# Last expert's down product and scatter, the gate half summed first, and the column offsets of the big tiles

## The chip, the cores and the metric

The kernel runs on one core of a Trainium2 chip. The metric is the device time of one execution in microseconds (us), lower being better. The kernel before was run three times: median 1566.77 us, from 1564.66 to 1566.87.

## The reference

One transformer block over a sequence of S = 256 rows with D = 2048 columns, all in fp32. A first part mixes a gated spatial unit and forgetting attention and adds its projection to the input; a second adds a mixture of experts. What matters here is the second:

```python
def hierarchical_moe(h, w_rg, b_rg, w_re, b_re, w_g, w_u, w_d):
    ...
    # one of 4 groups per row, then the best 2 of its 8 experts,
    # with gates w_top = softmax(top_v) * p_grp
    ...
    def expert_block(args):
        xi, e = args
        return (jax.nn.silu(xi @ w_g[e]) * (xi @ w_u[e])) @ w_d[e]
    ...
    y = y.at[buf_tok].add(yb * buf_gate[:, None])
```

There are 32 experts; `w_g` and `w_u` are 2048 x 512 each and `w_d` is 512 x 2048, so one expert has 12 MB of weights and all of them some 400 MB. Each row of the input goes to two experts and their results are added, times the row's gates.

## The kernel before, in words

The program has three stages, which are called the front, the expert stage and the tail below.

**The front** computes everything up to the router with products in split fp32r. `half` (L221 to L241) takes one weight tile of 128 partitions x 8 x 512, which a DMA of 2 MB brought, and for each of its eight 512-column slices makes a high part on ACT (L230) and the rest on DVE (L231). The two go by turns to a pair of 512-column tiles, either `wh` and `wl` or a pair cut out of the tile `ex` (`split_tiles`, L145). For each slice and each of the two 128-row blocks of the sequence TensorE makes three matmuls: high by high (L236), high by low (L237) and low by high (L238). The weights' part is what moves through TensorE, 512 columns at a time, and the 128x128 piece that is held comes from `hT`, `so` or `mT`, the transposed activations in split form. The profile calls the products `z<-wh,hT`, `z<-wl,hT`, `z<-ex,hT` and so on. The last projection goes in 256-column pieces.

Tiles are taken from pools on two sides of SBUF. On the left lie the two weight tiles `w0` and `w1` (the profile's `w`), the split tiles `wh` and `wl` and later `rb`; on the right `hT0`, `hT1`, `so0`, `so1`, `third`, `ex`, `bm`, `mT0`, `mT1`. In the built program each tile on the left begins at byte 416 of a 512-byte line (address modulo 512), each on the right at byte 480. The activations `x1`, which are read in the expert stage, begin at byte 128.

**The expert stage** streams the experts' weights, six tiles of 2 MB for each (two of gate, two of up, two of down), through the big tiles of the front as slots as these come free. `load` (L541) issues the next transfer on SP's queue whenever a slot is handed back: `used_up` is called after the last matmul that reads a slot. The loop over the experts is at L1020. For each, `hidden` makes the gate half and then the up half (16 matmuls each, four of them side by side in four column groups of the array, L861), `gather` prepares the next expert's rows, `silu_mul` (L866) copies the two results out of PSUM (gate on ACT, up on DVE, 512 columns each), sums and turns them by eight matmuls against `four` (L879), and makes `h` by a tanh on ACT and two DVE products (L881 to L884). `down` (L887) multiplies by the down weights, and after each fourth expert `scatter` (L997) adds the four results to the rows of the output `acc`, by a matmul against a 0/gate matrix `gt` and an addition on DVE. If some expert has more rows than its 32 places, `overflow` (L925) makes further passes; SP reads the number of those, `novi`, into a register for it.

**The tail** treats the last expert's down product apart. Its weights come in five column blocks, LAST = (0, 512), (512, 512), (1024, 512), (1536, 256), (1792, 256) as first column and width, each cut out of the usual rows of `w_expert_down`. `columns` (L903) makes the four partial products of a block (L908) and copies them to `yl` on ACT (L912), `add_columns` (L915) sums and spreads them by one fp32 matmul for each of the two row blocks (L920) against a matrix that holds the gates (`gq`, from `one_gates`, L845), and DVE adds the result to `acc` (L922). Then the block goes out. `keep_warm` (L158) issues matmuls on a constant, in numbers that the table WARM sets: WARM[1] = 20 of them before the last four matmuls of the last up half, WARM[2] = 10 behind it, WARM[3] = 10 before the first column block.

PE, DVE and ACT each run their instructions in the order that a scheduler wrote for them, SP its transfers likewise.

Of the kernel before, what the change touches and what calls it, by code (L numbers as in the profile page):

```python
# [9 lines left out]
F32 = mybir.dt.float32  # L10
F32R = mybir.dt.float32r
BF16 = mybir.dt.bfloat16
I32 = mybir.dt.int32
# [30 lines left out]
def hybrid_block(ctx: ExitStack, tc: tile.TileContext, a, out, dbg=None):  # L44
# [61 lines left out]
    def early(pool, name, dt=F32R):  # L106
        return pool.tile([P, QW], dt, tag=name, name=name)

    def wide_tile(pool, name, dt=F32R):
        return pool.tile([P, HW], dt, tag=name, name=name)  # L110

    def halves(pool, name):

# [427 lines left out]
    def load(n=1):  # L541


        while n and free and order:
            n -= 1
            t = order.popleft()
            slot[t] = free.popleft()
            w = slot[t][0]
            e, m, c = t // 6, t // 2 % 3, t % 2
            src = a[names[m]][e * P:(e + 1) * P]  # L550
            if t < last:
                n0 = HW // len(w)
                for i, wi in enumerate(w):
                    nc.sync.dma_start(wi, src[:, c * HW + i * n0:c * HW + (i + 1) * n0])
            else:
                sv = src.rearrange("p (j n) -> p j n", j=4)
                for c0, n0 in LAST:
                    if c0 // 1024 == c:
                        wv = quarter(t, c0 // 512 % 2).rearrange("p (j n) -> p j n", j=4)
                        nc.sync.dma_start(wv[:, :, c0 % 512:c0 % 512 + n0], sv[:, :, c0:c0 + n0])  # L560

    def quarter(t, c):

        w = slot[t][0]
        return w[c] if len(w) == 2 else w[0][:, c * QW:(c + 1) * QW]

    def room(tiles, keep=True):

# [258 lines left out]
    def turned(eq, tag):  # L827
# [4 lines left out]
        gt = mo.tile([P, S], F32, tag=tag, name="gt")  # L832
        nc.vector.tensor_copy(gt, gt_ps[:, :S])
        return gt

# [9 lines left out]
    def one_gates(pos, g, tag):  # L845

        eq = mo.tile([P, NT, 4, CAP], F32, tag="eq", name="eq")
        for tb in range(NT):
            ts(eq[:, tb], iota1.unsqueeze(1).to_broadcast([P, 4, CAP]), pos(tb), g(tb), ALU.is_equal, ALU.mult)
        return turned(eq, tag)  # L850

    def hidden(xT, t, piece=None):

        ps = gup.tile([P, 512], F32, tag="gu", name="ps")
        for c in range(4):
            if piece is None and t == last - 2 and c == 3:
                keep_warm(WARM[1])
            w = quarter(t + c // 2, c % 2) if piece is None else piece(c)
            w = w.rearrange("p (i d) -> p i d", i=4)
            for i in range(4):  # L860
                nc.tensor.matmul(ps[32 * i:32 * i + 32], xT[:, i, c], w[:, i], start=(c == 0), stop=(c == 3))  # L861
            if piece is None and c % 2:
                used_up(t + c // 2)
        return ps

    def silu_mul(g_ps, u_ps):  # L866


        s_ps = trm.tile([P, 512], F32, tag="tr", name="s_ps")
        both = []  # L870
        for i, ps in enumerate((g_ps, u_ps)):
            q = mo.tile([P, 512], F32, tag="xg", name="q")
            if i:
                nc.vector.tensor_copy(q, ps)  # L874
            else:
                nc.scalar.activation(q, ps, AF.Copy)
            both.append(s_ps[:, i * P:(i + 1) * P])
            for j in range(4):
                nc.tensor.matmul(both[i][:, j * CAP:(j + 1) * CAP], q[:, j * P:(j + 1) * P], four, start=True, stop=True)  # L879
        t = mo.tile([P, P], F32, tag="th", name="t")  # L880
        nc.scalar.activation(t, both[0], AF.Tanh, scale=0.5)  # L881
        stt(t, t, 1.0, both[0], ALU.add, ALU.mult)
        h = mo.tile([P, 4, CAP], F32, tag="h", name="h")
        stt(h.rearrange("p a b -> p (a b)"), t, 0.5, both[1], ALU.mult, ALU.mult)  # L884
        return h

    def down(h, t, p0):  # L887
# [12 lines left out]
            else:  # L900
                nc.vector.tensor_copy(o, i)  # L901

    def columns(h, w, tag):  # L903
# [5 lines left out]
        yl = mo.tile([P, 512], F32, tag=tag, name="yl", bufs=2 if tag == "xT" else 1)[:, :n]  # L909
        m = min(n, 256)  # L910
        for i in range(0, n, m):
            nc.scalar.activation(yl[:, i:i + m], y_ps[:, i:i + m], AF.Copy)  # L912
        return yl

    def add_columns(yl, gq, c0):  # L915

        n = yl.shape[1]
# [27 lines left out]
    def overflow_block(base, cum, ix, piof):  # L945
# [40 lines left out]
                return wo  # L986
            return f

        h = silu_mul(*(hidden(xo, None, piece(n)) for n in names[:2]))
        for c in range(4):  # L990
            wv = wo.rearrange("p (j n) -> p j n", j=4)
            for j in range(4):
                rows(wv[:, j], a["we_d"].rearrange("r (k n) -> (r k) n", n=512), row[:, 1 + j, c:c + 1])
            add_columns(columns(h, wv, "xg"), gq, c * 512)
        ts(ix, ix, 1.0, None, ALU.add)

    def scatter(q, gt, c):  # L997
# [22 lines left out]
    for e in range(NE):  # L1020
        q, el = divmod(e, 4)
        xT, t = nxt, 6 * e
        g_ps = hidden(xT, t)
        u_ps = hidden(xT, t + 2)
        if el == 0:
            gt = group_gates(q)
        if e < NE - 1:
            nxt = gather(e + 1)
        else:
            gq = one_gates(lambda tb: pos1[:, tb, e:e + 1], lambda tb: gw[:, tb, e:e + 1], "gq")  # L1030
            nc.gpsimd.memset(y[3 * CAP:], 0.0)
# [10 lines left out]
    yl = None  # L1042
    for i in range(len(LAST) + 1):
        nxt = None
        if i < len(LAST):
            c0, n = LAST[i]
            w = quarter(last + c0 // 1024, c0 // 512 % 2).rearrange("p (j n) -> p j n", j=4)[:, :, c0 % 512:c0 % 512 + n]
# [8 lines left out]
        yl = nxt  # L1056

def layout(inputs):  # L1060
# [19 lines left out]
    g0 = 5 * SW + NH  # L1080
    for n in range(4):
        order += [w[:, g0 + n * 512:g0 + (n + 1) * 512], w[:, g0 + D + n * 512:g0 + D + (n + 1) * 512]]
    wp = np.concatenate([g["w_proj_sgu"][0], g["w_proj_fox"][0]], axis=0)
    return {
        "x": c(x.reshape(NT, P, D).transpose(1, 0, 2)),
# [38 lines left out]
```

## Time and profile before

| what | value |
|---|---|
| median of three runs | 1566.77 us |
| the profiled execution | 1564.82 us |
| its span, first to last instruction | 1563.1 us |
| PE busy in the span | 1331.6 us (85%) |
| DVE busy | 578.4 us (37%) |
| ACT busy | 405.7 us (26%) |
| DMA rate over the span | 335 GB/s |
| mean granted TensorE clock | 0.916 |

The span is what the trace shows; the time of an execution is 1.7 us more than it. A busy share is an average over the three stages, which have different limits, so each stage is to be read by itself.

### The profile page before, as it was taken

What the parts mean: (1) busy time and instruction counts of PE and PEld (TensorE: products, weight loads), DVE (VectorE), ACT (ScalarE), POOL (GpSimd) and SP (SyncE); (2) the same over time, 40 slices, a digit from 0 to 9 for tenths busy, and PEclk for the clock granted to TensorE, in tenths of its full rate; (3) what the DMA queues carried; (4) which work ended last, traced back from release to release, by engine and by line L of the source; (5) the groups of instructions that cost most, each with busy time, mean ns of one, the idle gap of its engine ahead of it and who ended that gap; (6) DMA issues with size and microseconds to landing.
All of it is one profiled execution on the core that took longest, in us unless ns stands there. A gap on an engine that the chain in (4) does not pass through costs nothing. (4 is left out here: it accounts for less than half of the span.)

```text
span 1563.1 us, 18318 instructions
## 1 busy us (share of the span) xinstructions
PE 1331.6 (85%) x7506; PEld 749.6 (48%) x7506; DVE 578.4 (37%) x1089; ACT 405.7 (26%) x724; POOL 31.9 (2%) x38
## 2 busy tenths in 40 slices
PE   9999999999999999898766878768778668768667
PEld 7787888888888878533222322222222212222223
DVE  6766766655655655422112202112112112112112
ACT  6645455545445444111000100010010000000000
POOL 0300100000000000000000000000000000000000
PEclk9999999999999999999788979789778888889889
DMA  9554453455555955899999999999999999999996
GB/s 384 223 209 169 161 201 142 155 200 192 199 192 223 369 228 190 347 425 428 425 426 425 425 428 426 427 426 427 426 426 426 425 428 426 426 427 426 427 425 240
DMA packets 50375, 523.53 MB, mean 335 GB/s; under 512 B 5872, under 2 KB 11632, under 8 KB 16752
## 3 DMA queue, kind: packets, MB, share of 16 engines
q1 hardware_dynamic: 48992, 520.22, 80.7%
q10 hardware_dynamic: 1296, 2.11, 0.5%
q8 instruction: 60, 0.98, 0.2%
q14 instruction: 27, 0.22, 0.0%
HBM read 520.21 MB, written 2.10 MB: 334 GB/s over the span
## 5 line engine op out<-in xcount | busy, mean ns | idle before, releaser
L231 DVE TENSOR_TENSOR wl<-w,wh 128x512 fp32r<-128x512 f32 x220 | 151.0, 690 | 115.2 <-ACT wh L230 114.8
L230 ACT ACTIVATE wh<-w 128x512 fp32r<-128x512 f32 x220 | 138.0, 631 | 157.0 <-PE z L238 145.3
L874 DVE COPY q<-ps 128x512 f32<-128x512 f32 x32 | 22.1, 692 | 391.4 <-PE ps L861 385.3
L236 PE MATMUL z<-wh,hT 128*128 128x512 f32 x382 | 153.3, 402 | 0.8 <-ACT wh L230 0.8
L237 PE MATMUL z<-wl,hT 128*128 128x512 f32 x382 | 151.1, 396 | 2.3 <-DVE wl L231 2.3
L238 PE MATMUL z<-wh,hT 128*128 128x512 f32 x382 | 150.8, 395 | 0.0
L879 PEld LDWEIGHTS s_ps<-four,q 128*128 128x128 f32 x512 | 70.9, 214 | 117.7 <-DVE q L874 63.5
L879 PE MATMUL s_ps<-four,q 128*128 128x32 f32 x512 | 78.2, 300 | 46.5 <-DVE q L874 25.5
L899 ACT ACTIVATE mT<-y_ps 32x512 f32<-32x512 f32 x62 | 36.5, 589 | 278.3 <-DVE mT L901 278.3
L861 PE MATMUL ps<-hT,xT 128*32 128x512 f32 x512 | 76.6, 711 | 33.3 <-DMA hT<-in_we_u_dram 17.1
L861 PE MATMUL ps<-w,xT 128*32 128x512 f32 x512 | 80.1, 747 | 27.4 <-DMA w<-in_we_u_dram 22.7
L881 ACT ACTIVATE t<-s_ps 128x128 f32<-128x128 f32 x32 | 8.9, 278 | 320.8 <-PE s_ps L879 320.8
L816 PE MATMUL x_ps<-x,sel 128*32 128x512 f32 x512 | 90.1, 708 | 0.7 <-DVE sel L812 0.7
L237 PEld LDWEIGHTS z<-wl,hT 128*128 128x128 f32 x382 | 71.7, 188 | 19.9 <-DVE wl L231 4.2
L901 DVE COPY mT<-y_ps 32x512 f32<-32x512 f32 x62 | 42.4, 684 | 103.7 <-PE y_ps L892 83.4
L236 PEld LDWEIGHTS z<-wh,hT 128*128 128x128 f32 x382 | 71.6, 188 | 17.7 <-ACT wh L230 1.0
L238 PEld LDWEIGHTS z<-wh,hT 128*128 128x128 f32 x382 | 71.6, 187 | 17.2
L861 PE MATMUL ps<-third,xT 128*32 128x512 f32 x320 | 53.8, 740 | 26.7 <-DMA third<-in_we_u_dram 15.3
L236 PE MATMUL z<-ex,hT 128*128 128x512 f32 x194 | 76.4, 395 | 0.0
L237 PE MATMUL z<-ex,hT 128*128 128x512 f32 x194 | 76.0, 392 | 0.0
L238 PE MATMUL z<-ex,hT 128*128 128x512 f32 x194 | 75.8, 391 | 0.0
L861 PE MATMUL ps<-so,xT 128*32 128x512 f32 x352 | 56.0, 745 | 21.4 <-DMA so<-in_we_g_dram 19.0
(301 smaller groups left out, 1852.9 us busy)
## 6 DMA issues: line engine op xcount, KB each, us to landing
w<-in_we_u_dram SPq DMA_DIRECT2D x21, 2048.0 KB, 34.3
w<-in_w_in_dram SPq DMA_DIRECT2D x20, 2048.0 KB, 7.4
hT<-in_we_u_dram SPq DMA_DIRECT2D x20, 2048.0 KB, 34.3
so<-in_we_d_dram SPq DMA_DIRECT2D x20, 2048.0 KB, 34.3
third<-in_w_in_dram SPq DMA_DIRECT2D x14, 2048.0 KB, 7.3
hT<-in_we_g_dram SPq DMA_DIRECT2D x12, 2048.0 KB, 34.3
so<-in_we_u_dram SPq DMA_DIRECT2D x12, 2048.0 KB, 36.8
w<-in_we_g_dram SPq DMA_DIRECT2D x11, 2048.0 KB, 34.3
```

The source lines that it names most:

```text
L230: nc.scalar.activation(wh, wv, AF.Copy)
L231: nc.vector.tensor_tensor(wl, wv, wh.bitcast(F32), ALU.subtract)
L236: nc.tensor.matmul(z[tb], hi, wh[:, i - j], start=first, stop=False)
L237: nc.tensor.matmul(z[tb], hi, wl[:, i - j], start=False, stop=False)
L238: nc.tensor.matmul(z[tb], lo, wh[:, i - j], start=False, stop=final)
L816: nc.tensor.matmul(x_ps[32 * c:32 * c + 32], sel[:, tb], x1[:, tb, c * 512:(c + 1) * 512], start=(tb == 0), stop=(tb == NT - 1))
L861: nc.tensor.matmul(ps[32 * i:32 * i + 32], xT[:, i, c], w[:, i], start=(c == 0), stop=(c == 3))
L874: nc.vector.tensor_copy(q, ps)
L879: nc.tensor.matmul(both[i][:, j * CAP:(j + 1) * CAP], q[:, j * P:(j + 1) * P], four, start=True, stop=True)
L881: nc.scalar.activation(t, both[0], AF.Tanh, scale=0.5)
L899: nc.scalar.activation(o, i, AF.Copy)
L901: nc.vector.tensor_copy(o, i)
```

## The change

It has four parts.

1. The last expert's down weights come from a new array, `we_l`, which the host lays out so that each column block's row lies in one piece (8 KB or 4 KB for each partition, where it was four pieces of 2 KB or 1 KB).
2. For every expert the gate half is copied out, summed, turned and put through tanh ahead of the up half. Each half is copied by both engines, columns 0 to 255 by ACT and the rest by DVE. `group_gates` and the last `one_gates` move; the 20 constant matmuls inside the last up half and the 10 behind it go, and 6 stay ahead of the first column block.
3. In the tail a block's partial products are split into an fp32r high part (ACT) and the rest (DVE) in a tile `fine`, which takes the place of a slot, and two fp32r matmuls for each row block take the place of one in fp32. The matrix holds ones; the gate is applied where DVE adds to `acc`.
4. Two unused tiles of 8 fp32 (`pad`, `rpad`) are put in and `ii` gets its place in `low`. In the built program all big tiles, on both sides, then begin at byte 448 of a 512-byte line; `x1` stays at 128.

The number of experts' transfers, their size, the matmuls of the front and their order on every engine are the same as before.

```diff
-WARM = (45, 20, 10, 10, 4, 60, 0)
+WARM = (45, 20, 0, 6, 4, 60, 0)
...
+    ctile([P, 8], F32, "pad")
...
     bm = early(ra, "bm", F32)
+    ra.tile([P, 8], F32, tag="rpad", name="rpad")
...
-    ii = small.tile([P, CAP], I32, tag="ii", name="ii", bufs=1)
+    ii = low.rearrange("p a b -> p (a b)")[:, 0:CAP].bitcast(I32)
...
-                        wv = quarter(t, c0 // 512 % 2).rearrange("p (j n) -> p j n", j=4)
-                        nc.sync.dma_start(wv[:, :, c0 % 512:c0 % 512 + n0], sv[:, :, c0:c0 + n0])
+                        nc.sync.dma_start(block(c0, n0), a["we_l"][:, 4 * c0:4 * (c0 + n0)])
...
-            if piece is None and t == last - 2 and c == 3:
-                keep_warm(WARM[1])
...
+    def add_turned(o, ps):
+
+        q = mo.tile([P, 512], F32, tag="xg", name="q")
+        nc.scalar.activation(q[:, 0:256], ps[:, 0:256], AF.Copy)
+        nc.vector.tensor_copy(q[:, 256:], ps[:, 256:])
+        for j in range(4):
+            nc.tensor.matmul(o[:, j * CAP:(j + 1) * CAP], q[:, j * P:(j + 1) * P], four, start=True, stop=True)
...
+    def silu(g_ps):
 
         s_ps = trm.tile([P, 512], F32, tag="tr", name="s_ps")
...
+        g = s_ps[:, 0:P]
+        add_turned(g, g_ps)
         t = mo.tile([P, P], F32, tag="th", name="t")
+        nc.scalar.activation(t, g, AF.Tanh, scale=0.5)
+        stt(t, t, 1.0, g, ALU.add, ALU.mult)
+        return t, s_ps[:, P:2 * P]
+
+    def times_up(tu, u_ps):
+        t, u = tu
+        add_turned(u, u_ps)
         h = mo.tile([P, 4, CAP], F32, tag="h", name="h")
+        stt(h.rearrange("p a b -> p (a b)"), t, 0.5, u, ALU.mult, ALU.mult)
         return h
...
-    def add_columns(yl, gq, c0):
+    def add_columns(parts, gq, c0, gate=None):
...
-            keep(nc.tensor.matmul(ps, gq[:, tb * P:(tb + 1) * P], yl, start=True, stop=True))
+            for i, yl in enumerate(parts):
+                keep(nc.tensor.matmul(ps, gq[:, tb * P:(tb + 1) * P], yl, start=(i == 0), stop=(i == len(parts) - 1)))
             o = acc[tb][:, c0:c0 + n]
-            tt(o, o, ps, ALU.add)
+            if gate is None:
+                tt(o, o, ps, ALU.add)
+            else:
+                stt(o, ps, gate(tb), o, ALU.mult, ALU.add)
...
-        g_ps = hidden(xT, t)
+        if e == NE - 1:
+            gq = one_gates(lambda tb: pos1[:, tb, e:e + 1], None, "gq", F32R)
+            nc.gpsimd.memset(y[3 * CAP:], 0.0)
+        tu = silu(hidden(xT, t))
         u_ps = hidden(xT, t + 2)
-        if el == 0:
-            gt = group_gates(q)
...
-        h = silu_mul(g_ps, u_ps)
+        h = times_up(tu, u_ps)
+        if el == 0:
+            gt = group_gates(q)
...
-            nxt = columns(h, w, "xT")
+            y_ps = columns(h, block(c0, n).rearrange("p (j n) -> p j n", j=4))
+            nxt = [fine[:, 2 * c0 + k * n:2 * c0 + (k + 1) * n] for k in range(2)]
+            nc.scalar.activation(nxt[0], y_ps, AF.Copy)
+            tt(nxt[1], y_ps, nxt[0].bitcast(F32), ALU.subtract)
...
-            add_columns(yl, gq, c0)
+            add_columns(parts, gq, c0, lambda tb: gw[:, tb, NE - 1:NE])
...
+        "we_l": c(np.concatenate([wl[:, :, i:i + n].reshape(P, 4 * n) for i, n in LAST], axis=1)),
```

The order of SP's transfers at the start of the expert stage, where the first experts' weights are fetched. Before:

```order
L554 DMA w_121<-in_we_u_dram 128x4096
L554 DMA rb<-in_we_u_dram 128x4096
L554 DMA mT_5259<-in_we_d_dram 128x4096
L554 DMA hT_4181<-in_we_d_dram 128x4096
L554 DMA hT_4182<-in_we_g_dram 128x4096
```

And after:

```order
L561 DMA w_123<-in_we_u_dram 128x4096
L561 DMA rb<-in_we_u_dram 128x4096
L561 DMA mT_5260<-in_we_d_dram 128x4096
L942 TENSOR_LOAD novi
L942 ISA x2
L561 DMA hT_4182<-in_we_d_dram 128x4096
L561 DMA hT_4183<-in_we_g_dram 128x4096
```

The load of `novi` into a register, which stood 44 rows further down, ahead of a transfer to `third`, now stands ahead of the first transfer to `hT`.

DVE's last instructions, from the last expert's sums on. Before, the tail has two additions for each column block:

```order
L833 COPY gt<-gt_ps 128x256
L874 COPY q<-ps 128x512
L882 SCALAR_TENSOR_TENSOR t<-t,s_ps 128x128
L884 SCALAR_TENSOR_TENSOR h<-t,s_ps 128x128
L922 TENSOR_TENSOR mT_5066<-mT_5066,ps 128x512
L922 TENSOR_TENSOR mT_5259<-mT_5259,ps 128x512
```

And after, with `hT_9178` the tile `fine`, `mT_5067` and `mT_5260` the two row blocks of the output:

```order
L882 COPY q<-ps 128x256
L900 SCALAR_TENSOR_TENSOR h<-t,s_ps 128x128
L1073 TENSOR_TENSOR hT_9178<-y_ps,hT_9178 128x512
L938 SCALAR_TENSOR_TENSOR mT_5067<-ps,gw,mT_5067 128x512
L1073 TENSOR_TENSOR hT_9178<-y_ps,hT_9178 128x512
L938 SCALAR_TENSOR_TENSOR mT_5260<-ps,gw,mT_5260 128x512
L938 SCALAR_TENSOR_TENSOR mT_5067<-ps,gw,mT_5067 128x512
L1073 TENSOR_TENSOR hT_9178<-y_ps,hT_9178 128x512
L938 SCALAR_TENSOR_TENSOR mT_5260<-ps,gw,mT_5260 128x512
```

Each block has three DVE instructions in place of two, and those before `h` have become a copy of half the width and one product.

## Rows read from the trace of the kernel before

**Rows 1.** Busy time by stretch; columns as in the first line.

```profile
core 0: us, PE busy (x) PEld busy (x) DVE busy (x) ACT busy (x) POOL busy (x), PEclk, DMA share, GB/s
0.00:640.00 640.00, 633.39 (x3060) 513.36 (x3061) 396.02 (x717) 321.90 (x557) 30.07 (x37) 1.00 0.57 218
640.00:1536.00 896.00, 677.29 (x4313) 226.72 (x4317) 174.85 (x360) 80.73 (x158) 1.80 (x1) 0.86 1.00 423
...
1546.00:1548.00 2.00, 2.00 (x11) 0.34 (x11) 0.00 (x0) 0.01 (x1) 0.00 (x0) 0.50 0.02 5
```

**Rows 2.** Chain that ended last, in order of time: start us, us, what.

```profile
1501.35 34.41 DMA w<-in_we_u_dram
...
1535.80 1.06 PE ps L861 x8
1536.87 1.22 PE ps L158 x20
...
1542.73 1.09 PE s_ps L879 x8
...
1546.06 1.86 PE y_ps L908 x8
...
1549.44 1.91 PE ps L920 x4
1551.35 1.00 PE y_ps L908 x8
...
1559.69 0.42 DVE mT L922
```

**Rows 3.** Timeline around the front's end and SP's queue: start us, us, instruction.

```profile
643.20 0.15 DVE L1018 CAST novi<-nov 128x1 int32<-128x1 f32 x1
647.34 0.33 SPq L554 DMA_DIRECT2D hT<-in_we_d_dram  x1
...
810.60 0.33 SPq L554 DMA_DIRECT2D so<-in_we_u_dram  x1
813.13 0.33 SPq L554 DMA_DIRECT2D third<-in_we_u_dram  x1
```

**Rows 4.** Timeline of PE in the front, products from both kinds of split tile.

```profile
200.06 0.39 PE L236 MATMUL z<-wh,hT 128*128 128x512 f32 x1
...
203.56 0.39 PE L236 MATMUL z<-ex,hT 128*128 128x512 f32 x1
...
204.94 0.39 PE L236 MATMUL z<-ex,hT 128*128 128x512 f32 x1
...
206.30 0.39 PE L236 MATMUL z<-wh,hT 128*128 128x512 f32 x1
```

**Rows 5.** Front's first product by tile and shape: count, busy us, mean ns, idle before.

```profile
L236 PE MATMUL z<-wh,hT 128*128 128x512 f32 x382 | 153.3, 402 | 0.8 <-ACT wh L230 0.8
L236 PE MATMUL z<-ex,hT 128*128 128x512 f32 x194 | 76.4, 395 | 0.0
L236 PE MATMUL z<-wh,mT 128*128 128x512 f32 x88 | 35.6, 405 | 0.0
L236 PE MATMUL z<-wh,so 128*128 128x512 f32 x88 | 34.7, 394 | 0.0
...
L236 PE MATMUL z<-ex,so 128*128 128x512 f32 x40 | 15.6, 390 | 0.0
```

**Rows 6.** Timeline of weight loads in a scatter of the expert stage, one per matmul.

```profile
956.50 0.19 PEld L1001 LDWEIGHTS ps<-mT,gt 128*128 128x128 f32 x1 [0.24 <-issue]
956.93 0.19 PEld L1001 LDWEIGHTS ps<-mT,gt 128*128 128x128 f32 x1 [0.24 <-issue]
```

**Rows 7.** A DVE copy of 256 columns in the tail, from the timeline.

```profile
1539.49 0.42 DVE L833 COPY gt<-gt_ps 128x256 f32<-128x256 f32 x1 [7.87 <-PE gt_ps L831]
```

**Rows 8.** Groups by shape: instructions of 512 columns from PSUM to fp32r.

```profile
L530 DVE SCALAR_TENSOR_TENSOR mT<-ps,mT 128x512 fp32r<-128x512 f32 x8 | 5.5, 684 | 0.0
L529 ACT ACTIVATE mT<-ps 128x512 fp32r<-128x512 f32 x8 | 4.7, 583 | 0.0
```

More of the change, by code (lines that the diff above doesn't have):

```diff
@@ L107, in early @@
         return pool.tile([P, QW], dt, tag=name, name=name)
+    home = {}
     def wide_tile(pool, name, dt=F32R):
-        return pool.tile([P, HW], dt, tag=name, name=name)
+        t = pool.tile([P, HW], dt, tag=name, name=name)
+        home[id(t)] = pool, name
+        return t
     def halves(pool, name):
@@ L565, in quarter, with block @@
         return w[c] if len(w) == 2 else w[0][:, c * QW:(c + 1) * QW]
+    def block(c0, n0):
+        o = c0 % 512
+        return quarter(last + c0 // 1024, c0 // 512 % 2)[:, 4 * o:4 * (o + n0)]
     def room(tiles, keep=True):
@@ L825, in gather, with turned @@
         return xT
-    def turned(eq, tag):
+    def turned(eq, tag, dt=F32):
         gt_ps = trm.tile([P, 512], F32, tag="tr", name="gt_ps")
@@ L831, in turned @@
             nc.tensor.transpose(gt_ps[:, tb * P:(tb + 1) * P], eq[:, tb].rearrange("p a b -> p (a b)"), ident)
-        gt = mo.tile([P, S], F32, tag=tag, name="gt")
+        gt = mo.tile([P, S], dt, tag=tag, name="gt")
         nc.vector.tensor_copy(gt, gt_ps[:, :S])
@@ L843, in group_gates, with one_gates @@
         return turned(eq, "gt")
-    def one_gates(pos, g, tag):
+    def one_gates(pos, g, tag, dt=F32):
         eq = mo.tile([P, NT, 4, CAP], F32, tag="eq", name="eq")
         for tb in range(NT):
-            ts(eq[:, tb], iota1.unsqueeze(1).to_broadcast([P, 4, CAP]), pos(tb), g(tb), ALU.is_equal, ALU.mult)
-        return turned(eq, tag)
+            i1 = iota1.unsqueeze(1).to_broadcast([P, 4, CAP])
+            if g is None:
+                ts(eq[:, tb], i1, pos(tb), None, ALU.is_equal)
+            else:
+                ts(eq[:, tb], i1, pos(tb), g(tb), ALU.is_equal, ALU.mult)
+        return turned(eq, tag, dt)
     def hidden(xT, t, piece=None):
@@ L864, in hidden @@
         return ps
-    def silu_mul(g_ps, u_ps):
-        s_ps = trm.tile([P, 512], F32, tag="tr", name="s_ps")
[L870 to L879, printed above, removed]
-        t = mo.tile([P, P], F32, tag="th", name="t")
-        nc.scalar.activation(t, both[0], AF.Tanh, scale=0.5)
-        stt(t, t, 1.0, both[0], ALU.add, ALU.mult)
+    def add_turned(o, ps):
[5 more added lines that the diff above has]
+    def silu(g_ps):
+        s_ps = trm.tile([P, 512], F32, tag="tr", name="s_ps")
+        g = s_ps[:, 0:P]
+        add_turned(g, g_ps)
+        t = mo.tile([P, P], F32, tag="th", name="t")
+        nc.scalar.activation(t, g, AF.Tanh, scale=0.5)
[4 more added lines that the diff above has]
+        add_turned(u, u_ps)
         h = mo.tile([P, 4, CAP], F32, tag="h", name="h")
-        stt(h.rearrange("p a b -> p (a b)"), t, 0.5, both[1], ALU.mult, ALU.mult)
+        stt(h.rearrange("p a b -> p (a b)"), t, 0.5, u, ALU.mult, ALU.mult)
         return h
@@ L901, in down, with columns @@
                 nc.vector.tensor_copy(o, i)
-    def columns(h, w, tag):
+    def columns(h, w):
         n = w.shape[2]
@@ L908, in columns @@
             keep(nc.tensor.matmul(y_ps[32 * j:32 * j + 32], h[:, j], w[:, j], start=True, stop=True))
[L909 to L913, printed above, removed]
-    def add_columns(yl, gq, c0):
-        n = yl.shape[1]
+        return y_ps
+    def add_columns(parts, gq, c0, gate=None):
+        n = parts[0].shape[1]
         for tb in range(NT):
             ps = scm.tile([P, 512], F32, tag="sc", name="ps")[:, :n]
-            keep(nc.tensor.matmul(ps, gq[:, tb * P:(tb + 1) * P], yl, start=True, stop=True))
+            for i, yl in enumerate(parts):
+                keep(nc.tensor.matmul(ps, gq[:, tb * P:(tb + 1) * P], yl, start=(i == 0), stop=(i == len(parts) - 1)))
             o = acc[tb][:, c0:c0 + n]
-            tt(o, o, ps, ALU.add)
+            if gate is None:
+                tt(o, o, ps, ALU.add)
+            else:
+                stt(o, ps, gate(tb), o, ALU.mult, ALU.add)
     def overflow():
@@ L987, in piece @@
             return f
-        h = silu_mul(*(hidden(xo, None, piece(n)) for n in names[:2]))
+        tu = silu(hidden(xo, None, piece(names[0])))
+        h = times_up(tu, hidden(xo, None, piece(names[1])))
         for c in range(4):
@@ L993, in overflow_block @@
                 rows(wv[:, j], a["we_d"].rearrange("r (k n) -> (r k) n", n=512), row[:, 1 + j, c:c + 1])
-            add_columns(columns(h, wv, "xg"), gq, c * 512)
+            yo = mo.tile([P, 512], F32, tag="xg", name="yo")
+            nc.scalar.activation(yo, columns(h, wv), AF.Copy)
+            add_columns([yo], gq, c * 512)
         ts(ix, ix, 1.0, None, ALU.add)
@@ L1029, in hybrid_block @@
         else:
-            gq = one_gates(lambda tb: pos1[:, tb, e:e + 1], lambda tb: gw[:, tb, e:e + 1], "gq")
-            nc.gpsimd.memset(y[3 * CAP:], 0.0)
             keep_warm(WARM[2])
-        h = silu_mul(g_ps, u_ps)
+        h = times_up(tu, u_ps)
+        if el == 0:
+            gt = group_gates(q)
         if e < NE - 1:
@@ L1041, in hybrid_block @@
     keep_warm(WARM[3])
-    yl = None
+    pool, tag = home[id(slot[6 * (NE - 2) + 3][0][0])]
+    fine = wide_tile(pool, tag, F32R)
+    parts = None
     for i in range(len(LAST) + 1):
@@ L1046, in hybrid_block @@
             c0, n = LAST[i]
-            w = quarter(last + c0 // 1024, c0 // 512 % 2).rearrange("p (j n) -> p j n", j=4)[:, :, c0 % 512:c0 % 512 + n]
-            nxt = columns(h, w, "xT")
+            y_ps = columns(h, block(c0, n).rearrange("p (j n) -> p j n", j=4))
+            nxt = [fine[:, 2 * c0 + k * n:2 * c0 + (k + 1) * n] for k in range(2)]
+            nc.scalar.activation(nxt[0], y_ps, AF.Copy)
+            tt(nxt[1], y_ps, nxt[0].bitcast(F32), ALU.subtract)
             if i == 0:
@@ L1052, in hybrid_block @@
             c0, n = LAST[i - 1]
-            add_columns(yl, gq, c0)
+            add_columns(parts, gq, c0, lambda tb: gw[:, tb, NE - 1:NE])
             for tb in range(NT):
                 nc.sync.dma_start(out[tb * P:(tb + 1) * P, c0:c0 + n], acc[tb][:, c0:c0 + n])
-        yl = nxt
+        parts = nxt
 def layout(inputs):
@@ L1082, in layout @@
         order += [w[:, g0 + n * 512:g0 + (n + 1) * 512], w[:, g0 + D + n * 512:g0 + D + (n + 1) * 512]]
+    wl = g["w_expert_down"][0][NE - 1].reshape(4, P, D).transpose(1, 0, 2)
     wp = np.concatenate([g["w_proj_sgu"][0], g["w_proj_fox"][0]], axis=0)
```

1 line of the change is left out of this document (removed).

## The prediction, made before the changed kernel had run

> **What bounds the kernel now.** I read the busy time by stretch first, then the chain of waits backwards from the end. Up to 640 us PE is busy for 633.4 us at a granted clock of 1.00 while the DMA engines are busy 0.57 of the time: the front is bound by TensorE [rows 1]. From 640 to 1536 us DMA is busy all the time at 423 GB/s and PE only 677 of 896 us: the expert stage is bound by the stream of weights. The chain says the same: it steps from transfer to transfer, the last taking 34.41 us from its issue at 1501.35, since it stands behind some seven others, 2.097 MB / 423 GB/s = 4.96 us each [rows 1, 2]. That tile is the last up tile. It lands at 1535.76, and what follows is a chain of small steps on PE, ACT and DVE that ends with an addition at 1559.69 + 0.42 = 1560.11: the tail [rows 2]. The span ends 3.0 us behind that, with the last output transfer, which the change leaves as it is.
>
> So three things can move the time: PE's pace in the front, the start of the stream, and the length of the tail. Time saved on PE or DVE inside the expert stage is not seen.
>
> **The expert stage: nothing.** Summing the gate first puts a copy and four small matmuls between the two halves. That delays the release of an up tile by about a copy of 256 columns and half of a 1.09 us sum, some 1 us [rows 2, 7]; the cover is the queue of about 34 us [rows 2]. Without that cover it would be 1 us for each of 32 experts. One thing changes at the start: the load of `novi` goes ahead of the first transfer to `hT` on SP. `novi` is ready at 643.35 and that transfer starts at 647.34, so it has 4.0 us [rows 3]. In the old place the load and its branches stand between two issues that are 2.53 us apart [rows 3], and that bounds it. Cost 0, from 0 to 0.5. Everything behind it on SP, the whole stream, would be late by what it exceeds.
>
> **The tail: -8.3 us.** By the new order, from the landing at 1535.76:
> - the last up half, 16 matmuls as two groups of 1.06 without the 20 constant ones (1.22) between them: 1535.8 + 2.1 = 1537.9 [rows 2];
> - its copy, now 256 columns on each engine, 0.42: 1538.3 [rows 7]; the sum 1.09: 1539.4 [rows 2]; one DVE product of 128 columns, at most the copy's 0.4: 1539.8. Tanh and the first product are already done with the gate half;
> - 6 constant matmuls at 1.22 / 20 = 0.06: 1540.2; the first column block 1.00, as the second took at full clock [rows 2]: 1541.2;
> - ACT's high part, 0.58: 1541.8 [rows 8].
> From there DVE sets the pace. It has 3 instructions for each of three 512-column blocks at 0.684 and for each of two 256-column blocks at 0.42: 6.2 + 2.5 = 8.7 [rows 7, 8]. I add 0.7 for the first matmuls between its first subtraction and its first addition, and 15 hand-overs of 0.04 (an estimate from the gap between 1535.76 and 1535.80). The last addition ends at 1541.8 + 8.7 + 0.7 + 0.6 = 1551.8, against 1560.11: -8.3. PE needs 1.00 + 4 x 0.23 = 1.9 us for a wide block, just less than DVE's 2.05 [rows 2, 4, 8].
>
> The blocks' weights must not be late: 4 MB behind 1535.76 at 423 GB/s land at 1538.2, 1540.7 and 1543.2 for the wide ones [rows 1], and the first is wanted at 1540.2, the second at 1541.2. That is 0.5 us of cover; if packets of longer rows gain nothing, up to 1 us is lost. Bounds of the tail: -9.5 if the hand-overs cost nothing and copies overlap more, -4 if the clock falls (rival D).
>
> **The front: -11.2 us.** No instruction moves, but the tiles do: the moving operand `wh`, `wl` goes from byte 416 of its line, `ex` and the held `hT`, `so`, `mT` from 480, all to 448. The trace shows two paces. From 200.06 to 203.56 stand 15 matmuls from `wh` and `wl`: 233.3 ns each. From 204.94 to 206.30 stand 6 from `ex`: 226.7 ns [rows 4]. PE has no idle time to speak of beside them [rows 5], so pace is time. The slower kind are (382 + 88 + 88) x 3 = 1674, the faster (194 + 40) x 3 = 702 [rows 5]. What distinguishes the two is that `ex` lies at the same offset as the operand that is held, and `wh` does not, 64 bytes away. If the common offset is the cause, all run at 226.7 after the change: 1674 x 6.67 = 11.2 us less. The stream then starts earlier by as much, since its first transfer to `hT` waits for the front. No row shows a tile at 448, so the effect is bounded by the nearest rows: nothing if the two paces belong to the tiles and not to offsets, a step of 6.67 ns more (240) or less (220) either way, and below that the pace of the fp32 rows. I take 226.7, as that is the one row of a pair with equal offsets.
>
> An fp32 matmul of the expert stage, whose moving `mT` lies at 480 too, follows the one before it in 0.43 us, which is 214.5 for each time that 512 columns pass if they pass twice [rows 6]. By the Trainium skill, "TensorE: Matmul & The Clock Gate", section "Back-to-back issue gap", 512 columns take 512 / 2.4 + 2.5 = 216 ns alone and some 131 ns in a stream with weight loads. The trace disagrees with both: 233.3 and 226.7 in just such a stream. By 216 the front could get about 36 us shorter, an estimate from that page and the counts, which would be the direction of rival B. Against it speaks that the fp32 rows have their pace without any change of offset.
>
> **Sum.** 1564.82 - 8.3 - 11.2 = 1545.3 for an execution like the profiled one. The median of the three runs is 1.95 above that execution, so 1547.3 for the median; I say 1548 for half a microsecond of late blocks. A measurement of this kernel can tell about 0.2%, 3.1 us, from no change.
>
> **Rivals.**
> - Mid: the pace follows the moving tile's own offset, and 448 is halfway between 416 and 480: 230 ns for all. 1674 x 3.3 saved, 702 x 3.3 lost: -3.2, 1564.8 - 8.3 - 3.2 + 2.0 = 1555.3. For it: the same two paces [rows 4]. Against: nothing else.
> - N, the offsets do nothing: the paces belong to the kind of tile or to what ACT and DVE write beside it. Only the tail is left: 1558.5. The page "SBUF — State Buffer", section "Operand start alignment", says that alignment there is about legality, not speed, and that its runs timed nothing. By it alone one would forecast N; rows 4 show that two tiles of one shape and type do differ.
> - B, offsets that are multiples of 64 take the overhead away: 214.5 for all, 1674 x 18.8 + 702 x 12.2 = 40 us: 1518.6.
> - D, the tail gives only half: the clock was 0.50 from 1546 to 1548, behind sparse work on PE, and the column block in that time took 1.86 instead of 1.00 [rows 1, 2]. The change takes constant matmuls away and puts four matmuls for two in a block, so PE at half pace would be later than DVE: 4 us of the 8.3 lost, 1551.6.
> - C, slower: the conflict is with a neighbour of the new offset, and all front matmuls take one step more, 240 ns: 1674 x 6.7 + 702 x 13.3 = 20.5 lost, 1564.8 - 8.3 + 20.5 + 2.0 = 1579. It decides from a mean pace of 231.4 + 8.3 / 2376 = 234.9 ns up; between 233.6 and 236.2 the time would be called the same. For it: the paces differ in just such steps; against: both kinds show no 240 in these stretches [rows 4].
>
> **Chances.** Equal offsets (the forecast) 0.38, mid 0.24, N 0.10, D 0.08, B 0.09, C 0.11 (of which 0.04 comes out within 0.2%). Faster by over 0.2%: 0.38 + 0.24 + 0.10 + 0.08 + 0.09 = 0.89; the same 0.04; slower 0.07. The range takes in the forecast, mid, N and D and leaves out B and C, 0.20: from 1538 (one step lower in the slower kind's place for part of the front, with the tail's better bound) to 1560 (N with 1 us of late blocks).
>
> **What would show it.** The matmuls of the front from `wh` and from `ex` following each other at 226.7 ns both; the boundary between front and expert stage some 11 us earlier, with the same 4.96 us for each 2 MB behind it; the last up tile landing at 1524.6; the last addition 16 us behind that landing instead of 24.4, with DVE busy nearly without a gap in the last ten and the clock at 1.00. The forecast is wrong if the `wh` products keep 233 or move anywhere but to 227, if SP issues the first transfer to `hT` later against PE's last front matmul than before, or if the tail's blocks wait for DMA.

## The result, and the profile after

The changed kernel takes 1546.84 us (median of 4 runs, 1546.67 to 1547.14) against 1566.12 us before (4 runs): ratio 0.9878, 95% interval 0.9861 to 0.9895, 19.3 us less. The forecast was 1548.

The profiled execution has a span of 1545.0 us, 18.1 less than before. The trace divides these into three. The first transfer to `hT` starts at 638.36 instead of 647.34 [rows 3]: 9.0 us earlier. From there to the landing of the last up tile it takes 887.5 us instead of 888.4: 0.9. From that landing (1525.87) to the end of the last addition it takes 16.1 us instead of 24.35 [rows 2]: 8.2.

The front first. Two rows of PE's timeline after the change, in a stretch of products from `wh` and `wl` (start us, us, instruction):

```profile
196.17 0.39 PE L245 MATMUL z<-wh,hT 128*128 128x512 f32 x1
...
199.57 0.39 PE L245 MATMUL z<-wh,hT 128*128 128x512 f32 x1
```

Between them lie 15 matmuls: 3.40 / 15 = 226.7 ns, where [rows 4] gave 233.3 for the same kind. The products from `ex` settle at 226.7 before and after; the first few of them behind each change of tile took 230 before (in [rows 4] the six from 203.56 to 204.94) and now mostly do not. The groups by tile and shape, to hold against [rows 5]:

```profile
L243 PE MATMUL z<-wh,hT 128*128 128x512 f32 x382 | 151.6, 398 | 0.2 <-ACT wh L237 0.2
L243 PE MATMUL z<-ex,hT 128*128 128x512 f32 x194 | 76.1, 393 | 0.0
L243 PE MATMUL z<-wh,mT 128*128 128x512 f32 x88 | 35.2, 400 | 0.0
L243 PE MATMUL z<-wh,so 128*128 128x512 f32 x88 | 34.2, 389 | 0.0
L243 PE MATMUL z<-wh,mT 128*128 128x256 f32 x64 | 18.6, 290 | 0.0
```

The counts are the same, every mean for 512 columns is 2 to 5 ns shorter, and the one for 256 columns, which the prediction had left out, is 6 ns longer (it was 284). The mean of one matmul in such a row overlaps its neighbours; the pace is read from the starts.

The tail, from the chain of waits (start us, us, what) and two lines of the timeline:

```profile
1524.63 3.62 PE ps L873 x32
1528.70 1.10 PE s_ps L884 x8
1530.17 0.49 PE ps L165 x6
1530.67 1.00 PE y_ps L924 x8
1531.99 1.00 PE y_ps L924 x8
```

```profile
1525.91 0.13 PEld L873 LDWEIGHTS ps<-w,xT 128*32 128x32 f32 x4 [0.34 <-DMA w<-in_we_u_dram]
...
1541.12 0.87 DVE L938 SCALAR_TENSOR_TENSOR mT<-ps,gw,mT 128x256 f32<-128x256 f32 x2 [0.27 <-PE ps L933]
```

The first weight load for the last up tile comes at 1525.91, 0.04 us after the landing, while PE's matmuls on the tile ahead still run. In a second profile of the same kernel PE waited 0.86 us for the tile, and in the kernel before 2.93: its own work ahead of the tail is now nearly as late as the stream. One sum of 1.10 and not two stands behind the up half; the first column block starts 4.8 us behind the landing where it was 10.3 [rows 2], and takes 1.00, not 1.86. The last addition ends at 1541.12 + 0.87 = 1541.99.

The busy time of the expert stage and of two stretches of the tail (columns as in [rows 1]):

```profile
640.00:1522.00 882.00, 659.23 (x4225) 216.16 (x4224) 174.45 (x362) 84.46 (x187) 1.80 (x1) 0.88 1.01 426
...
1530.00:1532.00 2.00, 1.83 (x22) 0.78 (x25) 0.12 (x1) 0.27 (x1) 0.00 (x0) 1.00 0.53 221
...
1534.00:1538.00 4.00, 3.84 (x24) 1.42 (x24) 3.88 (x7) 0.98 (x2) 0.00 (x0) 1.00 0.56 211
```

The expert stage is still all DMA. In the tail the granted clock (seventh column) stays at 1.00, 2.4 GHz, where it was 0.50, 1.2 GHz, from 1546 to 1548 before [rows 1], and from 1534 to 1538 both PE (3.84 of 4) and DVE (3.88) are busy nearly all the time.

### The profile page after: what moved, and what is told of

It reads as the page before. It is cut to its first block, busy times and chain, and to the rows that moved or that the text cites. A ratio compares the mean times of both kernels' runs of the same rounds, so it can differ in the third digit from the quotient of the medians.

```text
span 1545.0 us, 18399 instructions
## 1 busy us (share of the span) xinstructions
PE 1309.3 (85%) x7472; PEld 741.7 (48%) x7472; DVE 586.4 (38%) x1126; ACT 410.6 (27%) x753; POOL 31.9 (2%) x38
## 4 chain that ended last, share of the span: by engine, by line
DMA 51%; PE 45%; DVE 2%; ACT 1%; issue 1%; POOL 0%; SPq 0%; DVEq 0%; ACTq 0%
DMA so<-in_we_d_dram 12%; DMA ex<-in_we_d_dram 12%; PE z L243 12%; PE z L244 12%; PE z L245 12%; DMA rb<-in_we_g_dram 9%; DMA w<-in_we_u_dram 9%; DMA hT<-in_we_g_dram 9%; PE ps L873 3%; PE ps L1020 1%; PE y_ps L908 1%; PE x_ps L826 1%; DVE wl L238 1%; PE s_ps L884 1%; ACT wh L237 0%
## 5 line engine op out<-in xcount | busy, mean ns | idle before, releaser
L243 PE MATMUL z<-wh,hT 128*128 128x512 f32 x382 | 151.6, 398 | 0.2 <-ACT wh L237 0.2
L245 PE MATMUL z<-wh,hT 128*128 128x512 f32 x382 | 149.1, 390 | 0.0
L881 ACT ACTIVATE q<-ps 128x256 f32<-128x256 f32 x64 | 24.5, 383 | 462.2 <-PE ps L873 459.5
L882 DVE COPY q<-ps 128x256 f32<-128x256 f32 x64 | 27.1, 424 | 273.1 <-ACT q L881 273.1
L884 PEld LDWEIGHTS s_ps<-four,q 128*128 128x128 f32 x512 | 64.8, 195 | 98.9 <-ACT q L881 96.2
L884 PE MATMUL s_ps<-four,q 128*128 128x32 f32 x512 | 72.1, 284 | 32.5 <-ACT q L881 32.5
L873 PE MATMUL ps<-w,xT 128*32 128x512 f32 x512 | 76.0, 674 | 24.8 <-DMA w<-in_we_g_dram 18.7
L873 PE MATMUL ps<-hT,xT 128*32 128x512 f32 x512 | 81.7, 725 | 17.9 <-DMA hT<-in_we_g_dram 14.1
L826 PE MATMUL x_ps<-x,sel 128*32 128x512 f32 x512 | 84.4, 656 | 0.7 <-DVE sel L822 0.7
L873 PE MATMUL ps<-so,xT 128*32 128x512 f32 x352 | 64.4, 818 | 19.6 <-DMA so<-in_we_g_dram 19.5
L238 DVE TENSOR_TENSOR wl<-third,wh 128x512 fp32r<-128x512 f32 x75 | 59.4, 801 | 34.1 <-ACT wh L237 34.1
```

What stands on the lines that cost most here:

```text
L238: nc.vector.tensor_tensor(wl, wv, wh.bitcast(F32), ALU.subtract)
L243: nc.tensor.matmul(z[tb], hi, wh[:, i - j], start=first, stop=False)
L245: nc.tensor.matmul(z[tb], lo, wh[:, i - j], start=False, stop=final)
L826: nc.tensor.matmul(x_ps[32 * c:32 * c + 32], sel[:, tb], x1[:, tb, c * 512:(c + 1) * 512], start=(tb == 0), stop=(tb == NT - 1))
L881: nc.scalar.activation(q[:, 0:256], ps[:, 0:256], AF.Copy)
L882: nc.vector.tensor_copy(q[:, 256:], ps[:, 256:])
```

## The experiments

Times are medians; "before" in the same jobs was 1565.65 to 1566.51.

**The two halves apart.** The changed kernel without its unused tiles puts the left side at byte 416 and the right at 480 again; every engine's order stays:

```diff
-    ctile([P, 8], F32, "pad")
...
-    ra.tile([P, 8], F32, tag="rpad", name="rpad")
```

> The changed kernel without its two unused tiles: weight tiles and split tiles on the left at byte 416 again, the right side at 480. Theory (equal offsets of the moving and the held operand give 226.7 ns, unequal ones 233.3): the products from wh and wl take 233.3 ns again, those from ex 226.7; the first transfer to hT about 9 us later than in the changed kernel, the tail as there (last addition 15.7 us behind the landing of the last up tile); time 1546.8 + 10.5 = about 1557. If the offsets were only a companion of the gain and the reordering were its cause, the front would stay at 226.7 and the time at 1547.

1557.14, ratio 0.9939 (0.9922 to 0.9955). `wh` and `wl` are at 233.3 again, `ex` settles at 226.7; the tail takes 15.8 us. The counterpart puts the tiles into the kernel before:

```diff
+    ctile([P, 8], F32, "pad")
...
+    ra.tile([P, 8], F32, tag="rpad", name="rpad")
...
-    ii = small.tile([P, CAP], I32, tag="ii", name="ii", bufs=1)
+    ii = low.rearrange("p a b -> p (a b)")[:, 0:CAP].bitcast(I32)
```

> The kernel before with the two unused tiles and ii inside low, nothing else: all big tiles at byte 448. Theory: all 512-column products of the front at 226.7 ns, the last up tile landing about 10 us earlier, the tail 24.4 us as before; time 1566.1 - 10.5 = about 1555.5. If the two parts of the change help each other, less than that here and less in the run without the tiles; if they simply add, the two gains sum to 19.3.

1557.22, ratio 0.9940 (0.9923 to 0.9956), where about 1555.5 was expected. The 512-column products settle at 226.7 (about one in nine of those from `wh` and `wl` takes 230 or more), the last up tile lands at 1525.26, the tail takes 24.9 us. This is the profile of the fastest execution, 1554.84; the other three took 1557.04 to 1557.44, and what made them longer is not known. The gains of the two by their medians, 9.3 and 9.2, come to 18.5 of the 19.3: within the spread of the four executions they add.

**Which offset it is.** The next two leave the program as it is and set the sizes of the two unused tiles, for 448 on the left and 480 on the right, and for 416 on both sides.

```diff
-    ra.tile([P, 8], F32, tag="rpad", name="rpad")
```

> The changed kernel with the left tile kept and the right one left out: moving wh and wl at byte 448, ex and all that is held at 480. Equal-offset theory: wh and wl at 233.3 ns (offsets differ by 32), ex at 226.7, time about 1557. Rival (the moving operand's own offset: 416 is slow, 448 and 480 are not): all at 226.7, time about 1547.

1557.8. PE's timeline:

```profile
197.44 0.40 PE L242 MATMUL z<-wh,hT 128*128 128x512 f32 x1
...
199.54 0.40 PE L242 MATMUL z<-wh,hT 128*128 128x512 f32 x1
```

Nine matmuls in 2.10 us, 233.3 each, with the moving operand at the very byte, 448, at which it had 226.7 in the changed kernel.

```diff
-    ctile([P, 8], F32, "pad")
...
-    ra.tile([P, 8], F32, tag="rpad", name="rpad")
+    ra.tile([P, 16], F32, tag="rpad", name="rpad")
```

> The changed kernel with all big tiles at byte 416 on both sides. Equal-offset theory: all products at 226.7 ns, time about 1547. Rival (own offset): all at 233.3 ns, those from ex too, front about 16 us longer than in the changed kernel, time about 1562.

1546.14. Its timeline, with the moving operand at 416 as before:

```profile
196.20 0.39 PE L242 MATMUL z<-wh,hT 128*128 128x512 f32 x1
...
199.60 0.39 PE L242 MATMUL z<-wh,hT 128*128 128x512 f32 x1
```

15 matmuls in 3.40 us: 226.7. So neither byte 416 nor a multiple of 64 matters by itself: 416 is slow against 480 and fast against 416, 448 slow against 480 and fast against 448. The rival of an own offset falls with both runs. All tiles of a side move together in every run, so that it is the held piece that has to match, and not another tile of its side, is the simplest reading and is not shown apart.

A larger distance, 128 bytes:

```diff
-    ctile([P, 8], F32, "pad")
+    ctile([P, 40], F32, "pad")
```

> The changed kernel with the left tiles at byte 64 and the right at 448, moving wh and wl 128 bytes past the held pieces' offset. Equal-offset theory: wh and wl at 233.3 ns or more, ex at 226.7, time about 1557. Rival (only small distances disturb, a larger one gives less than equality does): below 226.7 for wh and wl, time below 1546.

1555.87. The single gaps spread more (229 to 238 ns), with a mean near 233 for `wh` and `wl` and 228 to 229 for `ex`. A larger distance is no better than a small one; beyond 128 bytes it was not tried, so whether 256 bytes would count as equal is open.

**The parts of the tail.** Each is undone alone in the changed kernel. The rows of the last down weights:

```diff
-                        nc.sync.dma_start(block(c0, n0), a["we_l"][:, 4 * c0:4 * (c0 + n0)])
+                        sv = src.rearrange("p (j n) -> p j n", j=4)
+                        wv = quarter(t, c0 // 512 % 2).rearrange("p (j n) -> p j n", j=4)
+                        nc.sync.dma_start(wv[:, :, c0 % 512:c0 % 512 + n0], sv[:, :, c0:c0 + n0])
...
-            y_ps = columns(h, block(c0, n).rearrange("p (j n) -> p j n", j=4))
+            w = quarter(last + c0 // 1024, c0 // 512 % 2).rearrange("p (j n) -> p j n", j=4)[:, :, c0 % 512:c0 % 512 + n]
+            y_ps = columns(h, w)
```

> The changed kernel with the last expert's down weights fetched from the usual rows again (pieces of 2 KB and 1 KB). Theory: the transfers land some 0.2 to 1.5 us later, but only the second block's is near to what waits for it, so the time is 1546.8 + 0 to 0.5. Rival (the longer rows carry a good part of the tail's gain): 2 us or more slower.

1547.19: 0.35 more than the changed kernel, no difference that can be told. The transfers do land later, the wide blocks 2.67, 2.62 and 2.63 us apart against 2.49, 2.45 and 2.49, and the third block's matmuls then wait for their weights:

```profile
1506.98 27.46 DMA hT<-in_we_d_dram
1534.44 0.14 issue
1534.58 1.06 PE y_ps L926 x8
```

DVE is still at work on the block ahead of it, so the end hardly moves: landing to last addition is 16.0 us, against 16.1 and 15.8 in the two profiles of the changed kernel.

The order of gate and up:

```diff
-WARM = (45, 20, 0, 6, 4, 60, 0)
+WARM = (45, 20, 10, 10, 4, 60, 0)
...
-        tu = silu(hidden(xT, t))
+        g_ps = hidden(xT, t)
         u_ps = hidden(xT, t + 2)
...
-        h = times_up(tu, u_ps)
+        h = silu_mul(g_ps, u_ps)
```

> The changed kernel with the sums of gate and up both behind the up half for every expert, copies of 512 columns on one engine each, and the constant matmuls of before (20, 10 and 10). Theory: this carries most of the tail's gain: from the landing of the last up tile to the first column block 10.3 us as before instead of 4.8, so 5.5 us more, and with the clock at half for the first block as before about 1 us on top: 1546.8 + 5.5 to 6.5 = 1552.3 to 1553.3. Nothing is to be seen in the expert stage (a tile every 4.9 us).

1555.05 (1552.74 to 1555.70): 8.2 more, where 5.5 to 6.5 were expected. The chain and the busy time by stretch:

```profile
1535.82 1.25 PE ps L165 x10
1537.07 1.87 PE y_ps L921 x8
1538.93 0.54 PE ps L165 x4
1539.47 1.87 PE y_ps L921 x8
1541.34 1.43 PE ps L930 x4
```

```profile
1533.00:1536.00 3.00, 1.26 (x10) 1.15 (x11) 1.25 (x3) 0.28 (x1) 0.00 (x0) 0.86 0.16 61
1536.00:1542.00 6.00, 6.00 (x32) 2.19 (x31) 0.69 (x1) 1.19 (x2) 0.00 (x0) 0.50 0.00 0
```

PE had been busy for 1.26 of 3 us, and then the clock was 0.50 for six: both first blocks took 1.87 and the scatter behind them was slow too, more than the one block of before. The run that followed was to take the clock out of the difference. It keeps the old order and puts constant matmuls where PE had waited (the edit against the run above):

```diff
-WARM = (45, 20, 10, 10, 4, 60, 0)
+WARM = (45, 20, 10, 0, 4, 60, 0)
...
-    def silu_mul(g_ps, u_ps):
+    def silu_mul(g_ps, u_ps, warm=(0, 0)):
...
                 nc.tensor.matmul(both[i][:, j * CAP:(j + 1) * CAP], q[:, j * P:(j + 1) * P], four, start=True, stop=True)
+            if warm[i]:
+                wp = yp.tile([P, 512], F32, tag="y", name="ps")[:, :P]
+                for _ in range(warm[i]):
+                    keep(nc.tensor.matmul(wp, onesb, onesb, start=True, stop=True))
...
-        h = silu_mul(g_ps, u_ps)
+        h = silu_mul(g_ps, u_ps, (12, 16) if e == NE - 1 else (0, 0))
```

> The run with the old order of gate and up again (1555.05), but with constant matmuls laid into the two gaps of PE between the sums: 12 behind the gate's sum, 16 behind the up half's, in place of the 10 ahead of the first column block. Theory (about 3 us of the 8.2 that the old order costs are the clock at half in the first blocks: two blocks of 1.87 instead of 1.00 and a slow scatter): first blocks at 1.00, clock 1.00 up to the end, 1552. Rival (the order's length alone costs 8): 1555, whatever the clock.

1552.62, as the theory had it.

```profile
1534.00:1536.00 2.00, 1.82 (x25) 1.72 (x24) 0.52 (x2) 0.28 (x1) 0.00 (x0) 1.00 0.13 53
1536.00:1540.00 4.00, 3.88 (x33) 1.49 (x34) 1.52 (x3) 1.20 (x2) 0.00 (x0) 1.00 0.00 0
```

From 1530 on the clock stays at 1.00, and landing to last addition is 22.0 us, against 25.2 in the run before and 16.1 in the changed kernel. But the clock is not wholly out of the difference. In both runs PE waits some 2.9 us for the last up tile, and the up half behind that is slow. The chain and two stretches of this run:

```profile
1525.80 1.34 PE ps L875 x8
1527.14 2.25 PE ps L165 x20
1529.39 1.25 PE ps L875 x8
```

```profile
1526.00:1528.00 2.00, 2.00 (x17) 0.93 (x10) 0.00 (x0) 0.00 (x0) 0.00 (x0) 0.62 0.88 360
1528.00:1530.00 2.00, 2.00 (x17) 1.32 (x19) 0.00 (x0) 0.00 (x0) 0.00 (x0) 0.53 0.64 266
```

These steps take 4.84 us here and 4.59 in the run before, for 1.06 + 1.22 + 1.00 = 3.28 at full clock [rows 2]. (The kernel before had the same wait, 2.93 us, and kept its clock there; why it fell here is not shown.) So of the 9.1 us between 25.2 and 16.1, the old order itself is 22.0 - 1.6 - 16.1 = 4.3, where 1.6 is what the up half lost here. The ten constant matmuls ahead of the first block, left out here, are 1.25. The rest is the clock: 1.3 in the up half, and 2.2 from the first block to the last addition (13.6 us in the run before, 11.4 here, 11.3 in the changed kernel).

The fp32 scatter:

```diff
-            gq = one_gates(lambda tb: pos1[:, tb, e:e + 1], None, "gq", F32R)
+            gq = one_gates(lambda tb: pos1[:, tb, e:e + 1], lambda tb: gw[:, tb, e:e + 1], "gq")
...
-    pool, tag = home[id(slot[6 * (NE - 2) + 3][0][0])]
-    fine = wide_tile(pool, tag, F32R)
...
-            nxt = [fine[:, 2 * c0 + k * n:2 * c0 + (k + 1) * n] for k in range(2)]
-            nc.scalar.activation(nxt[0], y_ps, AF.Copy)
-            tt(nxt[1], y_ps, nxt[0].bitcast(F32), ALU.subtract)
+            yl = mo.tile([P, 512], F32, tag="xT", name="yl", bufs=2)[:, :n]
+            for k in range(0, n, 256):
+                nc.scalar.activation(yl[:, k:k + 256], y_ps[:, k:k + 256], AF.Copy)
+            nxt = [yl]
...
-            add_columns(parts, gq, c0, lambda tb: gw[:, tb, NE - 1:NE])
+            add_columns(parts, gq, c0)
```

> The changed kernel with the last scatter in fp32 again: one copy to yl, one fp32 matmul for each row block, gates in the matrix, a plain addition. Theory: from the first column block to the last addition it takes 12.0 us by PE alone at full clock (3 x (1.0 + 1.9) + 2 x (0.6 + 1.1)) where the fp32r form takes 10.9; 1546.8 + 1.1 = 1548. Rival (its gain in the comparison with before, 3.1 us, is all its own): 1550. The clock at 1.00 in the first block is the sign of the theory, as the sum ahead of it is short now.

1548.68: 1.8 more (1.1 by the theory, 3.1 by the rival), nearer to the theory. The chain of waits:

```profile
1531.04 0.99 PE y_ps L924 x8
1532.03 0.33 PE ps L165 x4
1532.36 0.99 PE y_ps L924 x8
1533.36 1.92 PE ps L933 x4
1535.27 0.99 PE y_ps L924 x8
1536.27 1.92 PE ps L933 x4
```

PE alone now carries it, block by block at full clock, 1.92 for a wide scatter where the changed kernel has 1.12 (its chain: 1532.99, 1.12). From the first block to the last addition it takes 13.0 us here, 14.05 before with the clock at half for the first block, and 11.3 in the changed kernel: of the 2.7 between before and the changed kernel about 1.0 is the clock and 1.7 the fp32r form.

The last constant matmuls:

```diff
-WARM = (45, 20, 0, 6, 4, 60, 0)
+WARM = (45, 20, 0, 0, 0, 60, 0)
```

> The changed kernel without the 6 constant matmuls ahead of the first column block and the 4 behind it. Theory (the dense up half just ahead holds the clock): the clock stays at 1.00 in the blocks and 0.5 to 0.9 us are saved, 1546 to 1546.3, no difference that can be told. Rival (those ten are what holds it): the clock falls to 0.50 in the blocks and the time is 1549 or more.

1546.35, with the clock at 1.00 in every stretch of the tail: the ten are not what holds it. Whether they may go for good was then asked together with byte 416 on both sides, beside the changed kernel on the same chip.

> The changed kernel once more, as the measure for the next run on the same chip: 1546.8.

> The changed kernel with all big tiles at byte 416 and without the ten constant matmuls at the tail. If the two small differences seen (0.7 for 416, 0.5 for the constants) are real and add, 1545.6; if they were scatter between runs, the same as the changed kernel, 1546.8. Either way no more than 1.2 us, below what one run can tell.

1546.77 and 1546.23 (1545.77 to 1550.39): the same. No version here is shown to beat the changed kernel.

## Why the prediction was right

**Front, -11.2: right in its cause, two too large.** The rule taken from two rows, equal offsets 226.7 and unequal 233.3 [rows 4], held in all cases that were run: three pairs of equal offsets (448, 416, and `ex` against the held tiles at 480) and three of unequal ones (416 against 480, 448 against 480, 64 against 448), each of these with `ex` settling near 227 in the same run. The rivals "mid", N and C asked for 230, 233 or 240 at the new offset, and B for 214.5; none was seen as a settled pace. From its first product to its last the front took 625.1 us before and 616.0 after: 9.1 less, and 9.4 less than in the run without the unused tiles (625.4). What the term lacked is the last projection: it had left out the 192 products of 256 columns, and these became slower, when settled by 6.7 ns each and in the mean by 5.6 (117.2 to 122.8 between starts), 1.1 us in all. The paces below come from PE's timeline of the kernel before and after it:

```profile
620.70 0.28 PE L238 MATMUL z<-wh,mT 128*128 128x256 f32 x1
...
626.14 0.28 PE L238 MATMUL z<-wh,mT 128*128 128x256 f32 x1
```

```profile
610.31 0.28 PE L243 MATMUL z<-wh,mT 128*128 128x256 f32 x1
...
611.99 0.28 PE L245 MATMUL z<-wh,mT 128*128 128x256 f32 x1
```

48 matmuls in 5.44 us are 113.3 ns each, 14 in 1.68 us are 120.0. Some `wh` products also follow at 231 to 236 (their mean is 227.5), which takes another microsecond. The products from `ex`, which the prediction took at 226.7 throughout, went the other way: their mean fell from 228.9 to 227.1, which saved 1.3 us. That leaves about 1 us of the missing two without a known cause.

**Expert stage, 0: right in sum, by luck.** The prediction gave the load of `novi`, now ahead of the first transfer to `hT`, 0 to 0.5 us, since `novi` is ready 4.0 us before that transfer. It named as a sign of being wrong that SP issues this transfer later against PE's last front matmul than before, and so it came. The last front matmul and the transfer, from the timelines of the kernel before (its transfer is at 647.34 [rows 3]), of the kernel before with the tiles moved, and of the changed kernel:

```profile
631.81 0.28 PE L238 MATMUL z<-wh,mT 128*128 128x256 f32 x1
```

```profile
622.09 0.28 PE L241 MATMUL z<-wh,mT 128*128 128x256 f32 x1
...
637.61 0.33 SPq L557 DMA_DIRECT2D hT<-in_we_d_dram  x1
```

```profile
622.19 0.28 PE L245 MATMUL z<-wh,mT 128*128 128x256 f32 x1
...
633.45 0.14 DVE L1037 CAST novi<-nov 128x1 int32<-128x1 f32 x1
...
638.36 0.33 SPq L561 DMA_DIRECT2D hT<-in_we_d_dram  x1
```

And the changed kernel's busy time just ahead of the transfer:

```profile
634.00:638.00 4.00, 4.00 (x36) 1.59 (x37) 1.38 (x4) 0.00 (x0) 0.00 (x0) 1.00 0.04 14
```

With the load in its old place the transfer starts 15.53 and 15.52 us behind the last front matmul, and so it does in the two runs with the old order of gate and up. With the load ahead it starts 16.17 behind it, and 4.91 behind the start of the cast that makes `novi`. In all ten profiles that have the load ahead it is these 4.9 us, and 16.2 or 16.7 behind the matmul. So the 4.0 us were too few: the transfer starts 0.64 us later here, and up to 1.18 later in others, where `novi` itself came half a microsecond later. The DMA engines are busy 0.04 of the time from 634 to 638, so no transfer on the way hides it. The last up tile lands 903.7 us behind the last front matmul here, and 903.2 in the three profiles with equal offsets and the load in its old place; the three with the 1.18 and equal offsets have 904.1. No run has the new order with the load in its old place, so a gain of half a microsecond from that is not shown.

Against this stands a stream that is 0.9 us shorter from the first transfer to `hT` to the last landing. It goes with the right side's offset: 888.4 to 888.9 in the three profiles with byte 480 there, 887.3 to 887.7 in the eleven with 448 or 416. Why is open.

**Tail, -8.3: right, step by step.** From the landing, forecast and measured: up half done 2.1 and 2.4, `h` 4.0 and 4.3, first block begun 4.4 and 4.8, its high part done 6.0 and 6.5, last addition 16.0 and 16.1. The first steps were each a little long: PE was still busy with the tile ahead when the last one landed (in the changed kernel's second profile it was not, and the first block began at 4.4, the last addition ended at 15.8). DVE's part, taken as 10.0 us, was shorter: 1541.99 - 1532.33 = 9.7. That DVE alone sets the pace is not borne out: in that time DVE is busy for 8.4 us and PE for 8.3, the chain steps between the two, and a wide block costs PE 1.00 + 1.12 = 2.1 us and not 1.9.

Rival D (the clock falls, half of the gain is lost) did not come in. What it took for the danger, the constant matmuls taken away, does not matter here (1546.35 without any). What is left as the reason, argued from these runs and not tested by itself, is the short way from the up half to the first block: 1.9 us in the run without constants, with a sum of 1.1 in it and the clock at 1.00, although PE had waited 1.06 us for the last up tile; 7.0 us with the old order, in which the clock fell.

**The sum.** The 1548 holds 1.95 us because the median before lay that much above the profiled execution, and half a microsecond for late blocks. The changed kernel's median lies 0.2 above its profiled execution and no block came late. That makes up for the two microseconds that the front fell short, so that the sum came within 1.2 us is in part luck.

How the parts share the tail's 8.2 us could not have been read from a sum, since they hang together by the clock. With the old order the fp32r scatter shows no gain from landing to end: 25.2 us, against 24.9 with the fp32 scatter (the kernel before with the tiles moved); the lost clock takes it. With the clock at 1.00 it is worth about the same in either order: from the first block to the last addition 13.0 us with the fp32 scatter, 11.4 with the fp32r form in the old order, 11.3 in the new.

**What stays open.** Why equal offsets help the long products and hurt the short ones, and what sets the 226.7 that is left at equal offsets; why the first transfer to `hT` comes 4.9 us behind `novi`. No run here tells it.

## What to carry to other kernels

Where two kinds of the same matmul follow each other at two paces, compare the addresses of what moves and of what is held, modulo 512 bytes; here two unused tiles of 32 bytes gave 9 us of 1566 without one instruction moved, and they should be tried on the shape that has the most products. Hold the first transfer of a stream against the last matmul of the stage ahead of it, in every version: that is how half a microsecond of a reordered load shows, which the start of the transfer by itself does not. In a chain at the end of a stream, take out of it what does not need the last tile; it can pay twice, as here, where the clock also stayed at 1.00 in the steps that followed. What a part of such a chain is worth has to be asked with the other parts in place and with the clock of every stretch beside it.

## What the runs showed of the hardware that was not expected

- The pace of 512-column fp32r matmuls depends on how the moving operand and the held piece lie to each other modulo 512 bytes: settled, 226.7 ns at distance 0 (both at 416, or 448, or 480), about 233 at 32, 64 and 128. A distance of 256 was not tried.
- With 256 columns distance 0 is the slowest: 120.0 ns, against 113.3 at distance 64 and about 118 and 119 at 32 and 128 (the runs with 448 against 480 and 64 against 448).
- After a stretch in which PE was busy 1.26 of 3 us the granted clock was 0.50 for 6 us; with constant matmuls in the same gaps (1.82 of 2 us busy) it stayed at 1.00. In the same two runs it also fell to 0.50 and 0.53 behind a wait of PE of 2.9 us for the last up tile.
- A register load on SP's queue, set ahead of a transfer, held that transfer until 4.9 us behind the instruction that made the value, in ten profiles out of ten.
